# Memory values 2 ahead of the mixer's output projection, memory keys 2 behind it, and an order laid out with the DMA queue as an engine

## The chip, the cores and the metric

One core of one Trainium2 chip runs one program. The time is device microseconds (us) of one execution. Engines: TensorE (PE in the profile, its weight loads PEld), VectorE (DVE), ScalarE (ACT), GpSimd (POOL) and SyncE (SP), which here only issues DMAs.

## The reference, cut to what matters

One layer of a streaming encoder on 512 prompt tokens and 64 sample tokens, 1024 features wide, in float32:

```python
x = x + mixer(rmsnorm(x))                  # gated DeltaNet and GLA branches, merged, then merged @ w_o
k, v = m @ w_k, m @ w_v                    # m = rmsnorm(mem_prompt), 256 memory tokens, 4 heads of 256
x = x + (softmax(q @ k.T / 16) @ v) @ w_mo # q = rmsnorm(x) @ w_mq, head by head
x = x + conv_ffn(rmsnorm(x))               # up, causal convolution, silu gate, down
```

The memory's keys and values (`k`, `v`) depend on `mem_prompt` and the weights alone, not on `x`, so their tiles can stand anywhere ahead of the attention head that reads them. They are outputs too (`o_mk`, `o_mv`).

## The kernel before, in words

Every float32 matrix product is made of three fp32r matmuls: each operand is split into a high part and the rest (`h`, `lo`), and high by high, high by rest and rest by high are summed in one PSUM bank. A 128 x 1024 weight tile comes from DRAM in a raw buffer (`wr`, 512 KB, a DMA issued on SP); ACT casts it to `h`, and `lo` is made in one of two ways. "Summed": ACT writes the negated high part and a DMA issued on POOL adds the weight from DRAM on top (`accumulate`, the rows `w<-wt` on POOL). Otherwise: ACT casts and DVE subtracts (`w<-wr,w`, `w<-ws,w`).

The output projection of the mixer (`wo`), the gates, the attention's output projection and most of the up projection work on pairs of tiles with seven products in place of eight (`products`, L1643): P1, P2, P3, Q4, Q5, Q6, Q7. Each product is 12 matmuls over 288 columns into one of three PSUM banks of the pair (bank a for P1, Q6, Q7 and Q4, b for Q5 and P3, c for P2). When a product is done, `wo_finish` (L1964) has DVE add the bank into the residual tile `x[m]` (`x<-sm,x`), and the next product on the same bank has to wait for that. The weights of P1, P2 and Q4 are quarters of the two raw tiles, made the summed way; those of Q5, Q6, P3 and Q7 are sums and differences of quarters, which DVE forms first (`ws`, from `wr`), then ACT casts and DVE subtracts.

The residual `x` has been overwritten by then, so `x_again` (L1953) loads it afresh, 8 tiles of 288 KB.

The stretch around the change is the list `ATT` (L123): one entry after another on TensorE. `("mk", i)` is one head's keys (two tiles of 24 matmuls, DVE evacuates them to `kraw`, which is stored to `o_mk` and split into `kvh` and `kvl`); `("mv", i)` is one head's values (48 matmuls in one bank, ACT evacuates to `vraw`, stored to `o_mv` and split likewise); `("wo", 0)` is all 28 products of the output projection; `("mq", i)` are queries. In the list, keys 2 stand directly ahead of `wo`, values 2 directly behind it.

The order of every engine's instructions is laid out ahead of time by `Driver` (L250). It runs through the program once, gives each instruction a start from costs per engine (`FIXED`, `PACE`, L255), and emits them in the order of these starts; on the chip each engine then runs its own list in order, and waits by semaphores. DMAs are in the same plan: `load` (L381) and `store` (L387) place a transfer on one resource "D" and put its issue 2.2 us ahead of that; `accumulate` (L393) is the DMA issued on POOL. The time at which the planner thinks that a load has landed decides how early ACT's and DVE's work on it stands in their lists. Issues on SP are in order as well: an issue that waits for its data (a store) or for a free buffer (a load, there are 5 raw buffers) holds up all behind it. `AFTER` (L126) says how many tiles of the down projection follow each pair of the up projection.

All recorded instructions have the line of one helper (L291), so the profile is read by tile names.

Of the kernel before, what the change touches and what calls it, by code (L numbers as in the profile page):

```python
# [14 lines left out]
ALU = mybir.AluOpType  # L15
# [3 lines left out]
D = 1024  # L19
# [18 lines left out]
HOP = 0.2  # L38
BACK = 6.0
MARGIN = 0.3  # L40
NWARM = 11


# [23 lines left out]
def weight_order():  # L67
# [7 lines left out]
    seq += [("out", m) for m in range(max(NB, 4), 8)]  # L75
    for kd, i in ATT:
        if kd == "wo":
# [22 lines left out]
def product_order(pairs, late=False):  # L100

    seq = []
    for i, pair in enumerate(pairs):
        now = [(pair, p) for p in (("P1", "P2", "Q5", "Q6", "P3", "Q7") if late and i == 0 else
                                   ("P1", "Q5", "Q6", "P3", "Q7", "P2", "Q4") if i == len(pairs) - 1 else
                                   ("P1", "Q5", "Q6", "P2", "P3", "Q7"))]
        if i:
            now.insert(2, (pairs[i - 1], "Q4"))  # L110
        seq += now
    return seq
# [7 lines left out]

WPAIRS = [(("wo", m), ("wo", m + 1)) for m in range(0, 8, 2)]

ATT = [("mk", 0), ("mv", 0), ("mv", 1), ("mk", 1), ("mk", 2), ("wo", 0), ("mv", 2), ("mk", 3), ("mq", 0), ("mq", 1), ("mq", 2), ("mq", 3), ("mv", 3)]  # L123
MPAIRS = [(("mo", m), ("mo", m + 1)) for m in range(2, 8, 2)]
JS = 4
AFTER = {7: 2, 8: 2, 9: 2, 10: 2, 13: 2, 14: 2, 15: 2, 16: 2, 20: 2, 21: 2}  # L126


def up_pair(j):
# [3 lines left out]
def ffn_order():  # L133

    seq, old = [("up", j) for j in range(JS)], []
    for j in range(JS, NJ):
# [3 lines left out]
        for i, q in ((j, "P1"), (j - 1, "Q7"), (j, "Q5"), (j, "P2"), (j - 1, "Q4"), (j, "Q6"), (j, "P3")):  # L140
            if i >= JS:
                seq.append(("upx", (i, q)))
        n = AFTER.get(j, 0)
        seq, old = seq + old[:n], old[n:]
# [36 lines left out]
def free(ap):  # L181
    n = 1
    for d in ap.shape[1:]:
        n *= d
    return n


class Engine:


    def __init__(self, drv, key, eng):
        self.drv, self.key, self.eng = drv, key, eng
# [4 lines left out]
    def weigh(self, calls):  # L197
        cost, aps, outs = 0.0, [], []
        for name, args, kw in calls:
# [5 lines left out]
            else:  # L205
                twice = self.key == "V" and len(ins) == 1 and self.port([(name, args, kw)])
                cost += self.drv.FIXED[self.key] + n * self.drv.PACE[self.key] * (0.5 if twice else 1.0)
            cost += 0.06 * (name == "scalar_tensor_tensor" or self.key == "V" and a[0].shape[-1] <= 128 and any(v.space == bass.MemoryType.PSUM for v in a[1:]))
# [41 lines left out]
class Driver:  # L250
# [1 line left out]

    FIXED = dict(V=0.15, A=0.17, G=0.2, D=0.01)  # L255
    PACE = dict(V=1 / 960, A=1 / 1180, G=1 / 465, D=512 / 320e3)

    def __init__(self, pe, sync):
        self.pe, self.sync = pe, sync
        self.chains = []  # L260
        self.done = set()
        self.now = 0.0
        self.half = self.type = None
        self.last = 0.0
        self.swapped = 0.0
        self.wrote = {}
        self.seen = {}
        self.ringed = {}
        self.busy = dict(V=[], A=[], G=[], D=[], port=[])
        self.ring = {}  # L270
        self.pending, self.fresh = set(), set()
        self.heap = []
        self.count = 0
        self.waiting = []
# [98 lines left out]
    def note(self, key, cost, outs, aps, fns, port=False):  # L373
# [4 lines left out]
        self.last = max(self.last, end)  # L378
        self.put(start, fns)

    def load(self, out, in_):  # L381
        cost = self.FIXED["D"] + free(out) * self.PACE["D"]
        start = self.place("D", max(self.ready_at(out), self.latest(self.seen, out)) + 2.2, cost)
        self.mark(self.wrote, start + cost, [out])
        self.put(start - 2.2, [(self.sync.dma_start, (out, in_), {})])

    def store(self, out, in_, issuer=None):  # L387
        cost = self.FIXED["D"] + free(in_) * self.PACE["D"]
        start = self.place("D", self.ready_at(in_) + 2.2, cost)
        self.mark(self.seen, start + cost, [in_])  # L390
        self.put(start - 2.2, [((issuer or self.sync).dma_start, (out, in_), {})])

    def accumulate(self, out, in_, issuer):  # L393

        issue = self.place("G", self.open([out], []), 1.0)
        cost = self.FIXED["D"] + 2 * free(out) * self.PACE["D"]
        end = self.place("D", issue + 2.0, cost) + cost + 1.0
        self.mark(self.wrote, end, [out])
        self.put(issue, [(issuer.dma_start, (out, in_), dict(accum_op=ALU.add))])

    def hold(self, fn, cost, args, kw):
        out, ins = args[0], args[1:]
# [38 lines left out]
    def advance(self, c):  # L441
        self.last = self.now
        r = next(c[1])
        if r is None:
            c[0] = self.last + MARGIN
        elif isinstance(r, list):
            c[0] = self.ready_at(*r) + MARGIN
        elif r != WAIT:
# [53 lines left out]
def tile_trunk(ctx, tc, xT, memT, wt, wd, vec, cst, w0, wgate, st_gdn, st_conv, st_gla, st_ffn, ckT, cv,  # L502
# [3 lines left out]
    V, A, G = Engine(drv, "V", nc.vector), Engine(drv, "A", nc.scalar), Engine(drv, "G", nc.gpsimd)  # L506
# [15 lines left out]
    def nm(s):  # L522
        cnt[0] += 1
        return f"{s}{cnt[0]}"
# [234 lines left out]
    for k in range(KT):  # L759
# [3 lines left out]
        if k in WPART:  # L763
            i, a, b = WPART[k]
# [917 lines left out]
    def xslot(i, s="x"):  # L1682

        return drv.rotate(f"F{i}", 1, fp.tile([P, SLOT], F32R if s != "x" else F32, tag=f"F{i}", name=nm(s), bufs=1))


    def main():
# [52 lines left out]
        for k in range(KT + 1):  # L1740
            for i, ps in enumerate(first2):
                j = k - i
# [210 lines left out]
        def x_again(m):  # L1953

            for i in (m, m + 1):
                x[i] = xslot(i)
                DMA(x[i][:, 0:T], xT[:, i, :])
# [4 lines left out]
        out = []  # L1962

        def wo_finish(pair, prod, a, b, c):  # L1964
            m = pair[0][1]
            xx, scale = (x[m], 0.5) if prod in ("P1", "Q6", "P3", "P2") else (x[m + 1], -0.5)
            half = N1 if prod in ("P1", "P2", "Q4") else N2
            V.scalar_tensor_tensor(xx[:, half], b if prod in ("Q5", "P3") else c if prod == "P2" else a, scale, xx[:, half],
                                   op0=ALU.mult, op1=ALU.add)
            if prod == ("P2" if m == 6 else "P3"):  # L1970
                drv.spawn(c_norm(m, C_GMEM, acc, out))
            elif prod == "Q4":
                drv.spawn(c_norm(m + 1, C_GMEM, acc, out))

        def c_norm(m, gcol, acc_, out_):
            yield [x[m]]
            sq_acc(acc_, x[m], m == 0)
            drv.done.add(("sq", m))
            if drv.ready(*(("sq", i) for i in range(8))):
                drv.spawn(c_rstat("n2", [(acc_, 0)], 4, True, 2.0))  # L1980
            while not drv.ready("wo"):
                yield WAIT
            out_.append((m, norm_prep(x[m], vcol(gcol + m))))
            drv.done.add(("norm", gcol, m))

        for kd, i in ATT:
            if kd == "mk":
                yield from mem_keys(i)
            elif kd == "mv":
                if i == 0:  # L1990
                    for j in range(0, 8, 2):
                        x_again(j)
                yield from mem_values(i)
            elif kd == "wo":
                yield tuple(("wop1", m) for m in range(1, 8, 2))
                yield from products(WPAIRS, [wops[m] for m in range(1, 8, 2)], wo_finish, tuple(("wops", m) for m in range(1, 8, 2)))
                drv.done.add("wo")
            else:
                if i == 0:
                    yield tuple(("norm", C_GMEM, m) for m in range(8))  # L2000
                    xs = xs_of([p for _, p in sorted(out, key=lambda t: t[0])])
                ckr, cvr = slot("ckr"), slot("cvr")
                DMA(r4(ckr[:, 0:512], 256), ckT[:, 2 * i:2 * i + 2, :])
                DMA(r4(cvr[:, 0:512], 256), cv[:, 256 * i:256 * i + 256].rearrange("(a p) d -> p a d", p=P))
                N["ks", i], N["vs", i] = split(ckr), cvr
                for m in (2 * i, 2 * i + 1):
                    b = []
                    yield from tile_proj("mq", m, xs, b)
                    if m == 0:
# [248 lines left out]
        for kd, i in FFN[:-1]:  # L2258
            if kd == "up":
                j = i  # L2260
# [22 lines left out]
            elif kd == "dn1":  # L2283
                m, p = i
# [85 lines left out]
        late, early = [(256, TP, 0), (TP, T, 256)], [(0, 128, 0), (128, 256, 128)]  # L2370
# [213 lines left out]
```

## Time and profile before

| | |
|---|---|
| median of 3 runs | 1089.2 us (1089.12 to 1092.17) |
| the profiled execution | 1091.1 us, its span (first to last instruction) 1089.3 us |
| PE busy | 1077.1 us, 99% of the span, 8278 matmuls |
| PEld busy | 1045.6 us |
| DVE / ACT / POOL busy | 748.4 / 705.9 / 363.1 us |
| DMA | 172.00 MB, mean 158 GB/s; SP's queue 98.26 MB, POOL's 71.84 MB |
| mean granted TensorE clock | 0.997 |

A row of a timeline gives the start, the duration until the last of a merged group ends, the engine, what is written and read, the count, and in brackets how long the engine stood idle before and who released it. The rows are pipelined: a matmul over 288 columns has a duration of 0.30 us, but the next one starts 0.13 us later. A row of windows gives, for a stretch, its length, each engine's busy time with its count, then the granted share of the TensorE clock, the share of the 16 DMA engines and GB/s.

### The profile page before, as it was taken

Reading aid. Unit: us, or ns where it says so; the run is one execution under the profiler, and the core shown is the slowest. Engines: PE = TensorE matmul, PEld = TensorE weight load, DVE = VectorE, ACT = ScalarE, POOL = GpSimd, SP = SyncE. Lnnn points to the kernel's source line nnn. Section 1 sums busy time; section 2 is a strip of 40 time slices with the busy share of each in tenths; the row PEclk is TensorE's granted clock in tenths of the full one; section 3 lists DMA queues with packets and bytes.
Section 4 is the critical chain, followed back from the end, with each engine's and each line's share of the span. In section 5 each row is a group of like instructions: output and inputs, shape, how many; then the busy total and the mean of one; then the engine's idle time right before and its main releaser. Section 6 shows DMA issues by size and latency. Waiting matters only on the chain.

```text
span 1089.3 us, 21589 instructions
## 1 busy us (share of the span) xinstructions
PE 1077.1 (99%) x8278; PEld 1045.6 (96%) x8278; DVE 748.4 (69%) x1460; ACT 705.9 (65%) x1404; POOL 363.1 (33%) x578
## 2 busy tenths in 40 slices
PE   9999999999999999989999999999999999999997
PEld 8999989998988999989999999999999999999997
DVE  6666845776756676886835767767877776778565
ACT  6675546564747577465755668767876776677645
POOL 1243216133624333123410125444343333332224
PEclk9999999999999999999999999999999999999999
DMA  9666345253337889686685258777789688788834
GB/s 302 148 155 149 60 102 138 60 123 83 83 79 150 199 223 194 243 243 163 154 241 148 49 123 194 176 167 150 168 194 196 146 212 186 172 169 183 201 77 112
DMA packets 68040, 172.00 MB, mean 158 GB/s; under 512 B 7905, under 2 KB 14177, under 8 KB 67937
## 3 DMA queue, kind: packets, MB, share of 16 engines
q0 software_dynamic: 30672, 71.84, 38.4%
q1 hardware_dynamic: 36976, 98.26, 27.6%
q8 instruction: 65, 1.06, 0.4%
q10 hardware_dynamic: 288, 0.52, 0.1%
q14 instruction: 39, 0.31, 0.1%
HBM read 158.15 MB, written 5.37 MB: 150 GB/s over the span
## 4 chain that ended last, share of the span: by engine, by line
PE 95%; DVE 1%; DMA 1%; ACT 1%; issue 0%; SPq 0%; ACTq 0%; DVEq 0%
PE sm L291 95%; DMA wr<-wt 1%; DMA x<-xT 0%; DVE w L291 0%; DVE acl L291 0%; ACT w L291 0%; DVE ql L291 0%; DVE ws L291 0%; SPq L291 0%; ACT ach L291 0%; ACT ao L291 0%; ACT vraw L291 0%; DVE q L291 0%; DVE xl L291 0%; ACT xh L291 0%
## 5 line engine op out<-in xcount | busy, mean ns | idle before, releaser
L291 PE MATMUL sm<-xh,w 128*128 128x290 f32 (+3 forms) x2304 | 445.4, 300 | 0.5 <-ACT w L291 0.4
L291 PEld LDWEIGHTS sm<-xh,w 128*128 128x128 f32 x2304 | 356.0, 189 | 5.1 <-issue 1.7
L291 PE MATMUL sm<-xl,w 128*128 128x290 f32 (+3 forms) x1152 | 270.2, 296 | 0.3 <-DVE xl L291 0.2
L291 POOL DMA_DIRECT2D w<-wt x153 | 135.4, 898 | 373.8 <-ACT w L291 284.2
L291 PE MATMUL sm<-ach,w 128*128 128x256 f32 (+1 forms) x1216 | 232.3, 297 | 3.8 <-DVE x L291 3.4
L291 PEld LDWEIGHTS sm<-xl,w 128*128 128x128 f32 x1152 | 200.5, 188 | 0.8 <-DVE xl L291 0.8
L291 PEld LDWEIGHTS sm<-ach,w 128*128 128x128 f32 x1216 | 191.2, 189 | 4.6 <-ACT w L291 3.6
L291 ACT CAST w<-wr 128x512 fp32r<-128x512 f32 (+5 forms) x207 | 158.7, 769 | 19.6 <-PE sm L291 18.1
L291 ACT ACTIVATE w<-wr 128x512 fp32r<-128x512 f32 (+5 forms) x186 | 143.0, 770 | 22.3 <-PE sm L291 19.1
L291 PE MATMUL sm<-acl,w 128*128 128x256 f32 (+1 forms) x608 | 147.1, 296 | 0.3 <-DVE acl L291 0.3
L291 ACT CAST w<-ws 128x512 fp32r<-128x512 f32 (+1 forms) x132 | 78.5, 603 | 47.9 <-DVE ws L291 27.4
L291 PEld LDWEIGHTS sm<-acl,w 128*128 128x128 f32 x608 | 108.1, 189 | 0.5 <-DVE acl L291 0.5
L291 DVE TENSOR_TENSOR w<-ws,w 128x512 fp32r<-128x512 f32 (+1 forms) x104 | 75.2, 731 | 20.5 <-ACT w L291 18.3
L291 DVE SCALAR_TENSOR_TENSOR fc<-fu,vec,fc 128x578 f32<-128x578 f32 x88 | 70.5, 815 | 3.0 <-ACT fc L291 2.9
L291 PE MATMUL sm<-sh,w 128*128 128x290 f32 x288 | 61.2, 297 | 0.0
L291 DVE TENSOR_TENSOR x<-x,sm 128x320 f32<-128x320 f32 (+3 forms) x95 | 38.7, 436 | 30.8 <-PE sm L291 30.5
L291 POOL DMA_DIRECT2D w<-wd x33 | 29.0, 899 | 64.9 <-ACT w L291 58.0
L291 ACT ACTIVATE fc<-fu,vec 128x578 f32<-128x578 f32 x44 | 38.1, 871 | 16.9 <-POOL fu L291 16.4
L291 PEld LDWEIGHTS sm<-sh,w 128*128 128x128 f32 x288 | 47.6, 189 | 0.0
L291 PE MATMUL sm<-oh,w 128*128 128x256 f32 (+1 forms) x256 | 44.7, 295 | 0.0
L291 DVE TENSOR_TENSOR ws<-ws,wr 128x512 f32<-128x512 f32 (+1 forms) x64 | 42.9, 670 | 1.1
L291 POOL DMA_DIRECT2D w<-ws x27 | 23.6, 874 | 50.7 <-ACT w L291 50.2
(388 smaller groups left out, 1958.4 us busy)
## 6 DMA issues: line engine op xcount, KB each, us to landing
wr<-wt SPq DMA_DIRECT2D x130, 512.0 KB, 5.8
w<-wt POOLq DMA_DIRECT2D x52, 512.0 KB, 6.5
w<-wt POOLq DMA_DIRECT2D x101, 256.0 KB, 6.1
w<-ws POOLq DMA_DIRECT2D x27, 256.0 KB, 5.2
x<-xT SPq DMA_DIRECT2D x16, 288.0 KB, 5.9
wr<-wd SPq DMA_DIRECT2D x8, 448.0 KB, 5.3
w<-wd POOLq DMA_DIRECT2D x8, 448.0 KB, 7.1
wr<-wt SPq DMA_DIRECT2D x12, 256.0 KB, 4.7
```

Of the source, the lines that this page charges most:

```text
L291: fn(*args, **kw)
```

## The change

The layout of the work changes in four places, and the planner's account of DMAs in one:

- `ATT`: values 2 change places with keys 2, so `("mv", 2)` stands ahead of `wo` and `("mk", 2)` behind it.
- The first pair of `wo` runs its products as P1, Q5, P2, Q6, P3, Q7 in place of P1, P2, Q5, Q6, P3, Q7.
- `x_again` loads only x[0] to x[3] when values 0 begin; x[4], x[5] are loaded when P1 of the first pair, x[6], x[7] when P1 of the second pair is handed to the planner.
- `AFTER` loses the entry of pair 20: two tiles of the down projection move behind pair 21.
- The planner: SP becomes an engine "S" on which an issue takes 0.55 us; a transfer of a 128 x 1024 tile takes 1.43 us on "D" from 2.0 us after the issue, and lands 1.0 us later; a store is issued 1.0 us after its data are ready (outputs y excepted). Before, a load counted as landed 2.2 us + 1.65 us after its issue, and issues cost nothing. An accumulating DMA is charged 1.2 in place of 2 transfers.

```diff
+STORE = 1.0
+ISSUE, LATENCY, LANDING = 0.55, 2.0, 1.0
...
-        now = [(pair, p) for p in (("P1", "P2", "Q5", "Q6", "P3", "Q7") if late and i == 0 else
+        now = [(pair, p) for p in (("P1", "Q5", "P2", "Q6", "P3", "Q7") if late and i == 0 and pair[0][0] in ('wo',) else
+                                   ("P1", "P2", "Q5", "Q6", "P3", "Q7") if late and i == 0 else
...
-ATT = [("mk", 0), ("mv", 0), ("mv", 1), ("mk", 1), ("mk", 2), ("wo", 0), ("mv", 2), ("mk", 3), ("mq", 0), ("mq", 1), ("mq", 2), ("mq", 3), ("mv", 3)]
+ATT = [("mk", 0), ("mv", 0), ("mv", 1), ("mk", 1), ("mv", 2), ("wo", 0), ("mk", 2), ("mk", 3), ("mq", 0), ("mq", 1), ("mq", 2), ("mq", 3), ("mv", 3)]
...
-AFTER = {7: 2, 8: 2, 9: 2, 10: 2, 13: 2, 14: 2, 15: 2, 16: 2, 20: 2, 21: 2}
+AFTER = {7: 2, 8: 2, 9: 2, 10: 2, 13: 2, 14: 2, 15: 2, 16: 2, 21: 2}
...
-    FIXED = dict(V=0.15, A=0.17, G=0.2, D=0.01)
-    PACE = dict(V=1 / 960, A=1 / 1180, G=1 / 465, D=512 / 320e3)
+    FIXED = dict(V=0.15, A=0.17, G=0.2)
+    PACE = dict(V=1 / 960, A=1 / 1180, G=1 / 465, D=0.0014)
...
+    def moved(self, issued, ap, times=1.0):
+
+        cost = times * free(ap) * self.PACE["D"]
+        return self.place("D", issued + LATENCY, cost) + cost
+
     def load(self, out, in_):
-        cost = self.FIXED["D"] + free(out) * self.PACE["D"]
-        start = self.place("D", max(self.ready_at(out), self.latest(self.seen, out)) + 2.2, cost)
-        self.mark(self.wrote, start + cost, [out])
-        self.put(start - 2.2, [(self.sync.dma_start, (out, in_), {})])
+        at = self.place("S", max(self.ready_at(out), self.latest(self.seen, out)) + HOP, ISSUE)
+        self.mark(self.wrote, self.moved(at + ISSUE, out) + LANDING, [out])
+        self.put(at, [(self.sync.dma_start, (out, in_), {})])
...
+        at = self.place("S" if issuer is None else "A", self.ready_at(in_) + (HOP if in_.tensor.name.startswith("yo") else STORE), ISSUE)
+        self.mark(self.seen, self.moved(at + ISSUE, in_) + LANDING, [in_])
+        self.put(at, [((issuer or self.sync).dma_start, (out, in_), {})])
...
         def wo_finish(pair, prod, a, b, c):
             m = pair[0][1]
+            if prod == "P1" and m < 4:
+                x_again(m + 4)
...
-                    for j in range(0, 8, 2):
+                    for j in range(0, 4, 2):
                         x_again(j)
```

What it does to the engines' lists, at the three places that matter below. SP's list from the load of the first pair's first raw tile on; `wr1149` and `wr1150` are the first pair's raw tiles, `wr1171` and `wr1172` the second pair's. Before:

```order
L291 DMA wr1149_6011<-wt 128x1024
L291 DMA o_mv<-vraw1130_5925 128x2x256
L291 DMA wr1150_6012<-wt 128x1024
L291 DMA o_mk<-kraw1142_6004 128x2x256
L291 DMA wr1171_6128<-wt 128x1024
L291 DMA wr1172_6129<-wt 128x1024
L291 DMA o_mk<-kraw1163_6086 128x2x256
L291 DMA wr1190_6307<-wt 128x1024
L291 DMA wr1191_6308<-wt 128x1024
L291 DMA wr1207_6414<-wt 128x1024
```

SP's list now, from the same tile on; here the second pair's raw tiles are `wr1172` and `wr1173`, and `x1168` to `x1194` are x[4] to x[7]:

```order
L294 DMA wr1149_6008<-wt 128x1024
L294 DMA o_mv<-vraw1119_5849 128x2x256
L294 DMA wr1150_6009<-wt 128x1024
L294 DMA o_mv<-vraw1130_5925 128x2x256
L294 DMA x1168_6173<-xT 128x576
L294 DMA x1169_6174<-xT 128x576
L294 DMA o_mk<-kraw1142_6001 128x2x256
L294 DMA wr1172_6177<-wt 128x1024
L294 DMA wr1173_6178<-wt 128x1024
L294 DMA o_mv<-vraw1159_6083 128x2x256
L294 DMA wr1187_6263<-wt 128x1024
L294 DMA wr1188_6264<-wt 128x1024
```

The first pair's second raw tile moved from behind the second store of values to ahead of it; the second pair's tiles still stand behind the store of keys 1; two loads of `x` came in.

DVE's list in the first pair of `wo`, from the read of P1's bank on. Bank names: `sm1177` is bank a, `sm1185` bank b, `sm1183` bank c. Before:

```order
L291 SCALAR_TENSOR_TENSOR x1113_5839<-sm1177_6165,x1113_5839 128x288
L291 TENSOR_TENSOR w1169_6126<-ws1170_6127,w1169_6126 128x512
L291 TENSOR_TENSOR kvl1176_6164<-kraw1163_6086,kvh1175_6163 128x512
L291 TENSOR_TENSOR ws1179_6187<-wr1172_6129 128x512
L291 TENSOR_TENSOR ws1182_6190<-ws1179_6187,wr1171_6128 128x512
L291 TENSOR_TENSOR w1178_6186<-ws1179_6187,w1178_6186 128x512
L291 TENSOR_TENSOR w1181_6189<-ws1182_6190,w1181_6189 128x512
L291 SCALAR_TENSOR_TENSOR x1113_5839<-sm1183_6191,x1113_5839 128x288
L291 SCALAR_TENSOR_TENSOR x1114_5840<-sm1185_6210,x1114_5840 128x288
L291 SCALAR_TENSOR_TENSOR x1113_5839<-sm1177_6165,x1113_5839 128x288
```

And now; `sm1167` is bank a, `sm1180` bank b, `sm1182` bank c:

```order
L294 SCALAR_TENSOR_TENSOR x1115_5845<-sm1167_6153,x1115_5845 128x288
L294 TENSOR_TENSOR w1170_6175<-ws1171_6176,w1170_6175 128x512
L294 SCALAR_TENSOR_TENSOR x1116_5846<-sm1180_6185,x1116_5846 128x288
L294 TENSOR_TENSOR ws1176_6181<-wr1173_6178 128x512
L294 TENSOR_TENSOR ws1179_6184<-ws1176_6181,wr1172_6177 128x512
L294 TENSOR_TENSOR w1175_6180<-ws1176_6181,w1175_6180 128x512
L294 TENSOR_TENSOR w1178_6183<-ws1179_6184,w1178_6183 128x512
L294 SCALAR_TENSOR_TENSOR x1115_5845<-sm1182_6207,x1115_5845 128x288
L294 TENSOR_TENSOR ws1184_6228<-ws1179_6184,wr1172_6177 128x512
L294 SCALAR_TENSOR_TENSOR x1115_5845<-sm1167_6153,x1115_5845 128x288
```

The read of bank b, on which P3 waits, moved from behind four operations on the second pair's raw tiles to ahead of all of them, and the operation on keys 2 (`kvl1176`) left.

POOL's list of accumulating DMAs: `w1151` is P1 of the first pair; `w1173` before and `w1174` now are P1 of the second pair; `w1180` before and `w1177` now Q4 of the first. Before:

```order
L291 DMA w1151_6013<-wt 128x512
L291 DMA w1157_6048<-wt 128x512
L291 DMA w1173_6130<-wt 128x512
L291 DMA w1180_6188<-wt 128x512
L291 DMA w1184_6209<-wt 128x512
L291 TENSOR_TENSOR ws1187_6230<-ws1182_6190,wr1171_6128 128x512
```

And now:

```order
L294 DMA w1151_6010<-wt 128x512
L294 DMA w1155_6049<-wt 128x512
L294 DMA w1177_6182<-wt 128x512
L294 DMA w1174_6179<-wt 128x512
L294 DMA w1181_6206<-wt 128x512
L294 DMA w1189_6265<-wt 128x512
```

P1 of the second pair moved from the third to the fourth place, behind Q4 of the first pair, and the sum that POOL formed went to DVE.

More of the change, by code (lines that the diff above doesn't have):

```diff
@@ L268, in __init__ @@
         self.ringed = {}
-        self.busy = dict(V=[], A=[], G=[], D=[], port=[])
+        self.busy = dict(V=[], A=[], G=[], D=[], S=[], port=[])
         self.ring = {}
@@ L379, in note @@
         self.put(start, fns)
+    def moved(self, issued, ap, times=1.0):
+        cost = times * free(ap) * self.PACE["D"]
+        return self.place("D", issued + LATENCY, cost) + cost
     def load(self, out, in_):
-        cost = self.FIXED["D"] + free(out) * self.PACE["D"]
-        start = self.place("D", max(self.ready_at(out), self.latest(self.seen, out)) + 2.2, cost)
-        self.mark(self.wrote, start + cost, [out])
-        self.put(start - 2.2, [(self.sync.dma_start, (out, in_), {})])
+        at = self.place("S", max(self.ready_at(out), self.latest(self.seen, out)) + HOP, ISSUE)
+        self.mark(self.wrote, self.moved(at + ISSUE, out) + LANDING, [out])
+        self.put(at, [(self.sync.dma_start, (out, in_), {})])
     def store(self, out, in_, issuer=None):
[L388 to L391, printed above, removed]
+        at = self.place("S" if issuer is None else "A", self.ready_at(in_) + (HOP if in_.tensor.name.startswith("yo") else STORE), ISSUE)
+        self.mark(self.seen, self.moved(at + ISSUE, in_) + LANDING, [in_])
+        self.put(at, [((issuer or self.sync).dma_start, (out, in_), {})])
     def accumulate(self, out, in_, issuer):
[L395 to L399, printed above, removed]
+        at = self.place("G", self.open([out], []), 0.9)
+        self.mark(self.wrote, self.moved(at + 0.9, out, 1.2) + LANDING, [out])
+        self.put(at, [(issuer.dma_start, (out, in_), dict(accum_op=ALU.add))])
     def hold(self, fn, cost, args, kw):
```

## The prediction

> **What bounds the kernel now.** I read the page's busy times first:
>
> ```profile
> span 1089.3 us, 21589 instructions
> PE 1077.1 (99%) x8278; PEld 1045.6 (96%) x8278; DVE 748.4 (69%) x1460; ACT 705.9 (65%) x1404; POOL 363.1 (33%) x578
> ```
>
> PE is busy for 1077.1 of 1089.3 us, and the change takes no matmul away. So it can win only what PE waits for, and lose only by new waits. The waits of PE come next: releaser, total, times, longest.
>
> ```profile
> PE sm L291 <- DVE x L291: 3.4, 1, 3.4
> PE sm L291 <- ACT ach L291: 0.5, 1, 0.5
> PE sm L291 <- ACT w L291: 0.4, 1, 0.4
> PE sm L291 <- DVE ql L291: 0.3, 1, 0.3
> PE sm L291 <- DVE acl L291: 0.3, 1, 0.3
> PE sm L291 <- DVE xl L291: 0.2, 1, 0.2
> ```
>
> One wait, 3.4 us, is twice as long as all others behind the program's start together (1.7). PE's timeline shows its place. Products follow each other by 1.60 us (479.00 to 480.60), so P3, the fifth of the first pair of `wo`, could begin at 479.00 + 4 x 1.60 = 485.40:
>
> ```profile
> 479.00 1.76 PE L291 MATMUL sm<-hl,w 128*128 128x288 f32 x12
> 480.60 0.30 PE L291 MATMUL sm<-ach,w 128*128 128x288 f32 x1
> ...
> 488.89 0.37 PE L291 MATMUL sm<-ach,w 128*128 128x288 f32 x1 [3.36 <-DVE x L291]
> ```
>
> It waits for DVE's read of its bank. The windows behind it (length; PE, PEld, DVE, ACT, POOL; granted clock, DMA share, GB/s) show a second loss:
>
> ```profile
> 488.90:491.50 2.60, 2.60 (x13) 2.60 (x14) 2.10 (x4) 0.62 (x1) 0.00 (x0) 0.60 1.09 282
> 491.50:493.70 2.20, 2.20 (x14) 2.20 (x14) 0.46 (x1) 1.73 (x3) 0.88 (x1) 0.70 0.97 304
> 493.70:495.30 1.60, 1.60 (x15) 1.60 (x14) 1.06 (x2) 0.24 (x1) 0.00 (x0) 1.00 0.59 102
> ```
>
> The clock granted was 0.60 for 2.60 us and 0.70 for 2.20 us: 2.60 x 0.40 + 2.20 x 0.30 = 1.04 + 0.66 = 1.70 us. The stall costs 3.36 + 1.70 = 5.06 us.
>
> Why did DVE read late? I follow four views backwards. SP's timeline:
>
> ```profile
> 474.98 0.39 SPq L291 DMA_DIRECT2D o_mk<-kraw  x1
> 475.42 1.42 SPq L291 DMA_DIRECT2D wr<-wt  x2
> ```
>
> The landing times of these two loads, each from the DMA issues of its own window (the last column is us from issue to landing):
>
> ```profile
> wr<-wt SPq DMA_DIRECT2D x1, 512.0 KB, 5.8
> ...
> wr<-wt SPq DMA_DIRECT2D x1, 512.0 KB, 6.5
> ```
>
> ACT's timeline:
>
> ```profile
> 481.35 0.63 ACT L291 ACTIVATE w<-wr 128x512 fp32r<-128x512 f32 x1 [1.52 <-DMA wr<-wt]
> ...
> 482.40 0.62 ACT L291 CAST w<-ws 128x512 fp32r<-128x512 f32 x1
> ```
>
> And DVE's:
>
> ```profile
> 480.80 0.46 DVE L291 SCALAR_TENSOR_TENSOR x<-sm,x 128x288 f32<-128x288 f32 x1
> 483.05 0.69 DVE L291 TENSOR_TENSOR w<-ws,w 128x512 fp32r<-128x512 f32 x1 [1.79 <-ACT w L291]
> 483.66 0.68 DVE L291 TENSOR_TENSOR kvl<-kraw,kvh 128x512 fp32r<-128x512 f32 x1
> 484.26 0.68 DVE L291 TENSOR_TENSOR ws<-wr 128x512 f32<-128x512 f32 x1
> 484.98 0.69 DVE L291 TENSOR_TENSOR ws<-ws,wr 128x512 f32<-128x512 f32 x1
> 485.65 2.36 DVE L291 TENSOR_TENSOR w<-ws,w 128x512 fp32r<-128x512 f32 x2
> 487.94 1.17 DVE L291 SCALAR_TENSOR_TENSOR x<-sm,x 128x288 f32<-128x288 f32 x3
> ```
>
> The second pair's raw tiles stand on SP behind the store of keys 1 (474.98) and land at about 481.2 (475.42 + 5.8) and 482.6 (the second is issued within the 1.42 of the row; its middle, 476.1, + 6.5). ACT's head of queue waits 1.52 us for the first, so its cast for the first pair's own weight comes at 482.40, and DVE idles 1.79 us. Then DVE's list holds six operations ahead of the reads, which come at 487.94 in place of 483.
>
> **The change part by part.** *The stall.* Of the seven DVE operations between 480.80 and the read of bank b, one is left ahead of it (the changed order, above); the operation on keys 2 is gone. Bank b is now written from 480.60 to 482.20, as Q5 comes second, and P3 still begins at 485.40. The read can start once DVE has the cast's result; even at the old 483.05, with 0.69 and 0.46, it ends at 484.2, 1.2 us early. So -3.36 - 1.70 = -5.06 us.
>
> What is late next? There are two places. First, Q7 (479.00 + 5 x 1.60 = 487.0) needs bank a, which is read behind all of the second pair's preparation. From the landing at 482.6: four operations by 0.6 to 0.7 (rows 483.66 to 485.65) to 485.3, the read of P2 0.46, another sum 0.69, the read of Q6 0.46: 486.9. This is just in time; a landing later by d costs d. I take 0, and as its bound 1.0, a little over the spread of the two landings (6.5 - 5.8 = 0.7).
>
> Second, P1 of the second pair, at 479.00 + 6 x 1.60 = 488.6. Its low part is needed 8 matmuls in, at 488.6 + 8 x 0.13 = 489.6, and comes by an accumulating DMA that now stands behind Q4's on POOL. Issued as now at about 482.3, it lands after 4.1 us (a quiet place) or 7.8 to 9.3 (this place now):
>
> ```profile
> 482.28 1.75 POOL L291 DMA_DIRECT2D w<-wt  x2 [7.75 <-ACT w L291]
> ```
>
> ```profile
> w<-wt POOLq DMA_DIRECT2D x1, 256.0 KB, 4.1
> ```
>
> ```profile
> DMA to landing us min/median/max: 7.8/8.5/9.3
> ```
>
> That is 486.4 to 491.6, so a wait of 0 to 2.0 us. The quiet place waits 0, the middle of the busy rows (8.5, so 490.8) 1.2; I find nothing that says which it is nearer to, and take the mean, 0.6 us.
>
> The Trainium skill, page "TensorE: Matmul & The Clock Gate", section "Part 1: The HAM clock gate", says the clock halves after an idle window of about 3.4 us and returns after as long a busy one. The trace agrees roughly (3.36 us of idling, then 4.8 us at 0.60 and 0.70, not a half); by that rule the short wait left here would cost itself alone.
>
> *Order of matmuls.* PE's list now changes 239 times, in place of 231, between fp32 matmuls of the gated stage and the others: 4 round trips. Such a place reads:
>
> ```profile
> 343.51 0.29 PE L291 MATMUL sm<-xh,w 128*128 128x288 f32 x1
> 343.63 0.29 PE L291 MATMUL sm<-xl,w 128*128 128x288 f32 x1
> 343.95 1.13 PE L291 MATMUL sm<-vg,kt 64*128 64x128 f32 x8
> ```
>
> 343.63 to 343.95 is 0.32 against 0.13 for a usual step: 0.19 us a trip at most, so 0 to 0.76 us; I take 0.4.
>
> *DVE.* Eight sums move from POOL to DVE: 8 x 0.69 = 5.5 us more on an engine busy 748.4 of 1089.3 us. PE hides them unless they stand ahead of a read it waits for; the only such place found is Q7's above. Cost 0; without that cover, 0.69 each.
>
> *x loads.* Four tiles come later, x[4] to x[7]. The store and load order on SP puts two of them ahead of the store of keys 1, so they delay no raw tile of the second pair unless they share its time on the DMA engines (the third rival).
>
> *AFTER, and the planner's numbers elsewhere.* PE has no wait there to win but the small rows (1.7 in all), and each could come back once: 0, bounds -1.1 and +1.1, as not all sit at one end.
>
> **Sum:** -3.36 - 1.70 + 0.6 + 0.4 = -4.06 us. The profiled execution (1091.1, span 1089.3, 1.8 around it) would go to 1087.0; the median of the runs shown is 1089.2, 1.9 below it, with the same order and so the same stall, and I forecast from it: **1085.1 us**. Ends: -5.06 with the small gains is 1083.0; with 1.0 at Q7 or P1, 0.76 of trips and part of the rest, 1087.0.
>
> **Rivals.** *First: the wait comes back at P1 of the second pair.* The accumulate lands as the slowest now, 9.3: wait 2.0, so 1089.2 - 5.06 + 2.0 + 0.4 = 1086.5, and up to 1.7 more if the clock drops, 1088.2. For: 7.8 to 9.3 now. Against: the quiet row, 4.1.
>
> *Second: the change doesn't do what it says.* The raw tiles still stand behind the store of keys 1, as before. If they hold ACT's head of queue as they do now and the wait moves on to Q7, where bank a is read behind their preparation, by as much as it has now (they would have to land 3.3 us later than now, since Q7 is just in time), the 5.06 stays: 1089.2 + 0.4 = 1089.6. For: the store of keys 1 stands ahead of them in both lists. Against: the operations left DVE's list ahead of the read.
>
> *Third, slower: loads of x collide with the accumulates.* Where all eight x loads run now, between 425 and 444, landings read:
>
> ```profile
> wr<-wt SPq DMA_DIRECT2D x6, 512.0 KB, 13.4
> x<-xT SPq DMA_DIRECT2D x8, 288.0 KB, 7.9
> ```
>
> against a usual raw load and accumulate (the page):
>
> ```profile
> w<-wt POOLq DMA_DIRECT2D x101, 256.0 KB, 6.1
> wr<-wt SPq DMA_DIRECT2D x130, 512.0 KB, 5.8
> ```
>
> A raw load there takes 13.4 / 5.8 = 2.3 times as long. If the moved loads do that to the accumulate, it lands 6.1 x 2.3 = 14.0 us after 482.3, at 496.3: wait 6.7, clock 1.7, so 1089.2 - 5.06 + 6.7 + 1.7 + 0.4 = 1092.9. It decides for slower by over 0.3% from a landing of 13.6 us. Against: only two x loads come near, not eight. The Trainium skill, page "DMA: Bandwidth & Descriptors", section "Issuing engines are not separate DMA queues", says transfers of SP and POOL share the 16 engines and interleave; the trace agrees (8.5 against 4.1), and by it this rival costs as worked out.
>
> **How the numbers follow.** A measurement of this kernel tells 0.3% from no change: 3.27 us, so faster is below 1085.9, slower above 1092.5. Forecast 0.62, first rival 0.16, second 0.10, third 0.12. Of the forecast's own range, 1083.0 to 1087.0, about four fifths lie below 1085.9: faster 0.62 x 0.8 = 0.50; same 0.12 + 0.16 + 0.10 = 0.38; slower 0.12. The range runs from 1083.0 over the second rival and a further 1.0 to 1090.6; it leaves out the third rival and little else.
>
> **What would show it.** Right: P3 begins without a wait, the clock reads 1.00 through the first two pairs, and what is left at Q7 or at the second P1 is under 1 us. Wrong: an accumulate that lands over 9.3 us after its issue, a wait of 3 us or more anywhere in `wo`, or new waits in the gated stage, where SP's list moved most and I put 0.

## The result, and the profile after

| | before | after |
|---|---|---|
| median of 6 runs | 1090.0 us (1088.8 to 1092.7) | 1101.1 us (1100.6 to 1102.8) |
| profiled execution, its span | 1091.1, 1089.3 us | 1100.8, 1099.0 us |
| mean granted clock | 0.997 | 0.996 |

The changed kernel is slower: ratio 1.0093, 95% interval 1.0080 to 1.0105. The forecast was 1085.1 us, in a range of 1083.0 to 1090.6. The head of the page after:

```profile
span 1099.0 us, 21611 instructions
PE 1080.6 (98%) x8278; PEld 1047.8 (95%) x8278; DVE 757.2 (69%) x1468; ACT 704.5 (64%) x1404; POOL 357.2 (32%) x570
```

The matmuls are as many as before, so I look for the loss in PE's waits and its clock. The waits of PE after (releaser, total, times, longest), those that are new or have changed:

```profile
PE sm L294 <- DMA w<-wt: 5.9, 2, 4.0
PE sm L294 <- DVE S L294: 1.1, 1, 1.1
PE sm L294 <- ACT gt L294: 1.1, 2, 0.7
...
PE sm L294 <- DVE gt L294: 0.9, 1, 0.9
...
PE sm L294 <- ACT qh L294: 0.4, 1, 0.4
PE sm L294 <- DMA w<-ws: 0.3, 1, 0.3
...
PE sm L294 <- DVE x L294: 0.2, 1, 0.2
```

The 3.4 us for DVE's read of x have become 0.2. In their place stand two waits for an accumulating DMA, 5.9 us, and a few small ones. To see where the time went, I take the first matmul of each stage from PE's timelines: memory keys, the attention's scores, the up projection, the norm's broadcast (`dg`) and the first one that reads `sl`. Before:

```profile
450.63 0.28 PE L291 MATMUL sm<-mh,w 128*128 128x256 f32 x1
558.25 0.28 PE L291 MATMUL sm<-kvh,qh 128*128 128x256 f32 x1
681.15 0.43 PE L291 MATMUL sm<-xh,w 128*128 128x290 f32 x2
700.06 0.97 PE L291 MATMUL sm<-dg,onesr 128*128 128x512 f32 x4
736.72 0.30 PE L291 MATMUL sm<-sl,w 128*128 128x290 f32 x1
```

And after, with the first matmul of `wo` (479.00 before):

```profile
454.66 0.28 PE L294 MATMUL sm<-mh,w 128*128 128x256 f32 x1
483.08 1.74 PE L294 MATMUL sm<-hl,w 128*128 128x288 f32 x12
561.35 0.28 PE L294 MATMUL sm<-kvh,qh 128*128 128x256 f32 x1
684.88 0.43 PE L294 MATMUL sm<-xh,w 128*128 128x290 f32 x2
708.13 1.23 PE L294 MATMUL sm<-dg,onesr 128*128 128x512 f32 x4
746.30 0.29 PE L294 MATMUL sm<-sl,w 128*128 128x290 f32 x1
```

The differences of neighbouring starts give each stage's length:

| stage | before | after | difference |
|---|---|---|---|
| up to the memory's keys (gated stages) | 450.63 | 454.66 | +4.03 |
| keys, values to the start of `wo` | 28.37 | 28.42 | +0.05 |
| `wo` to the scores | 79.25 | 78.27 | -0.98 |
| attention to the up projection | 122.90 | 123.53 | +0.63 |
| up projection to `dg` | 18.91 | 23.25 | +4.34 |
| `dg` to `sl` | 36.66 | 38.17 | +1.51 |
| from there to the span's end | 352.58 | 352.70 | +0.12 |

The sum is +9.7 us, the difference of the spans. Of that, 4.0 us lie ahead of everything that the list `ATT` moves, and 5.9 us lie about 200 us behind the start of `wo`. Of the attention's 0.63, 0.52 are one new wait for ACT (`qh`, at 603.74, from start to start). Stage lengths of the experiments are made in the same way, each from its own timeline.

**In `wo`** the wait moved on. PE's timeline, POOL's and SP's:

```profile
495.90 0.79 PE L294 MATMUL sm<-hl,w 128*128 128x288 f32 x4 [1.89 <-DMA w<-wt]
```

```profile
486.12 1.75 POOL L294 DMA_DIRECT2D w<-wt  x2 [8.08 <-DVE x L294]
```

```profile
485.59 0.90 SPq L294 DMA_DIRECT2D x<-xT  x2
```

The transfer waited for is the second of POOL's two, P1 of the second pair; the first is Q4's of the first pair. Two loads of x, x[6] and x[7], were issued just ahead of them, at 485.6. The landing times of POOL's two after their issue, and the window behind the wait in which the clock dropped:

```profile
DMA to landing us min/median/max: 7.8/8.5/9.2
```

```profile
496.94:500.35 3.41, 3.41 (x17) 3.41 (x16) 1.99 (x4) 0.45 (x1) 0.00 (x0) 0.50 1.07 299
```

A wait of 1.89 us is followed, 1 us later, by 3.41 us at a granted clock of 0.50: 3.41 x 0.50 = 1.71 us. Together that takes back 3.6 of the 5.06 us won.

**In the up projection** PE waits for the other accumulate:

```profile
707.49 0.80 PE L294 MATMUL sm<-xh,w 128*128 128x290 f32 x4 [4.01 <-DMA w<-wt]
```

POOL's timeline before, with the power operation `rt` of the norm, for which POOL waits for DVE:

```profile
687.35 0.88 POOL L291 DMA_DIRECT2D w<-wt  x1 [1.88 <-ACT w L291]
...
689.86 3.37 POOL L291 TENSOR_TENSOR rt<-rin,mhalf 128x5 f32<-128x5 f32 x1 [1.48 <-DVE rin L291]
693.19 1.81 POOL L291 DMA_DIRECT2D w<-wt  x2
```

And after:

```profile
693.59 4.11 POOL L294 TENSOR_TENSOR rt<-rin,mhalf 128x5 f32<-128x5 f32 x1 [4.31 <-DVE rin L294]
697.66 2.70 POOL L294 DMA_DIRECT2D w<-wt  x3
```

One of three accumulates, that of the weight `w1620`, has moved from ahead of `rt` to behind it. Counted from the first matmul of the up projection it is issued at 12.8 us in place of 6.2 (697.66 - 684.88 and 687.35 - 681.15). It then runs beside two others. The DMA issues, before and after (last column: us to landing):

```profile
w<-wt POOLq DMA_DIRECT2D x1, 512.0 KB, 5.2
```

```profile
w<-wt POOLq DMA_DIRECT2D x1, 512.0 KB, 9.8
```

Behind this wait the clock is at 0.50 for 3.41 us again, 1.71 us more:

```profile
708.56:711.97 3.41, 3.41 (x14) 3.18 (x14) 1.44 (x2) 2.47 (x4) 1.43 (x5) 0.50 1.07 238
```

**In the gated stages** PE has four new waits:

```profile
165.27 0.49 PE L294 MATMUL sm<-S,c 128*128 128x128 f32 x2 [1.12 <-DVE S L294]
305.86 0.34 PE L294 MATMUL sm<-keep,on 64*128 64x64 f32 x2 [0.89 <-DVE gt L294]
352.54 0.40 PE L294 MATMUL sm<-ach,w 128*128 128x288 f32 x1 [0.66 <-ACT gt L294]
424.31 0.40 PE L294 MATMUL sm<-ach,w 128*128 128x288 f32 x1 [0.40 <-ACT gt L294]
```

That is 3.07 us of idling. Measured from start to start against the usual step of such matmuls, they are 1.28, 1.05, 0.82 and 0.56 us, with one of 0.27 at 342.7: 3.98 together, of the stage's 4.03. The first has a plain cause. DVE's and POOL's timelines:

```profile
161.30 3.66 DVE L294 SCALAR_TENSOR_TENSOR z<-zt,z 128x576 f32<-128x576 f32 x1
164.88 0.33 DVE L294 SCALAR_TENSOR_TENSOR S<-S,dl,sm 128x128 f32<-128x128 f32 x1
```

```profile
160.86 1.38 POOL L294 TENSOR_TENSOR tg<-cst,ggh 128x512 fp32r<-128x512 f32 x1
161.88 1.36 POOL L294 TENSOR_TENSOR tg<-cst,ggl 128x512 fp32r<-128x512 f32 x1
162.88 1.45 POOL L294 TENSOR_TENSOR e<-gc 128x576 f32<-128x576 f32 x1
```

The gate z takes 3.66 us beside three POOL operations (the median of its kind is 0.76), and the state S, for which PE waits, stands behind it in DVE's list.

### The profile page after: what moved, and what is told of

Read it like the earlier page. It is cut to its first block, busy times and chain, and to the rows that moved or that the text cites. A ratio compares the mean times of both kernels' runs of the same rounds, so it can differ in the third digit from the quotient of the medians.

```text
span 1099.0 us, 21611 instructions
## 1 busy us (share of the span) xinstructions
PE 1080.6 (98%) x8278; PEld 1047.8 (95%) x8278; DVE 757.2 (69%) x1468; ACT 704.5 (64%) x1404; POOL 357.2 (32%) x570
## 4 chain that ended last, share of the span: by engine, by line
PE 91%; DMA 3%; DVE 2%; ACT 2%; issue 1%; POOL 0%; SPq 0%; POOLq 0%; ACTq 0%; DVEq 0%
PE sm L294 91%; DMA w<-wt 2%; DMA w<-ws 1%; ACT w L294 0%; DVE tu L294 0%; DMA x<-xT 0%; DVE z L294 0%; ACT gt L294 0%; ACT xh L294 0%; DVE w L294 0%; DVE ws L294 0%; ACT cx L294 0%; DVE xl L294 0%; DVE acl L294 0%; DVE x L294 0%
## 5 line engine op out<-in xcount | busy, mean ns | idle before, releaser
L294 DVE TENSOR_TENSOR w<-ws,w 128x512 fp32r<-128x512 f32 (+1 forms) x103 | 71.7, 705 | 24.9 <-ACT w L294 22.9
```

Of the source, the lines that this page charges most:

```text
L294: fn(*args, **kw)
```

## The experiments

Two theories were formed from these traces. Theory A: the planner's new figures cost the time, through the lists that they make, and the layout is good. Theory B: the layout (AFTER, the x loads) costs it. Ratios are to the kernel before on the same chip, with a 95% interval; its median there was 1091.5 us in each of the three groups of runs.

**Layout with the old planner.** The changed kernel, with the planner's figures and its load, store and accumulate as before.

```diff
-    PACE = dict(V=1 / 960, A=1 / 1180, G=1 / 465, D=0.0014)
+    PACE = dict(V=1 / 960, A=1 / 1180, G=1 / 465, D=512 / 320e3)
...
```

> The changed list, the new product order, the split x loads and AFTER, with the old planner's numbers. Theory A (the planner's new numbers cost the time, the layout is good): no wait of 4.0 us at the up projection, no new waits in the gated DeltaNet stage, the 3.4 us wait of wo gone: 1089.5 - 5 + 0.5 = about 1085, between 1083 and 1088. Theory B (the layout costs it, by AFTER and the moved loads): 1097 to 1101, with the 4.0 us wait still there.

1091.5 us, ratio 1.0003 (0.9995 to 1.0012). The 4.0 us wait and the gated stage's waits are gone, as theory A says; but the time lies in neither range, since the whole layout is worth nothing. PE still waits in `wo`, and once more in a later pair:

```profile
489.92 0.37 PE L294 MATMUL sm<-ach,w 128*128 128x288 f32 x1 [3.08 <-DVE x L294]
```

SP's timeline shows why:

```profile
475.12 1.54 SPq L294 DMA_DIRECT2D x<-xT  x2
476.71 0.46 SPq L294 DMA_DIRECT2D wr<-wt  x1
479.78 0.40 SPq L294 DMA_DIRECT2D o_mv<-vraw  x1
480.22 2.30 SPq L294 DMA_DIRECT2D wr<-wt  x3
```

The wait is at Q7 (due 8.0 us after the first matmul of `wo`, at 478.71 + 8.0 = 486.7). Two x loads now stand ahead of the second pair's raw tiles. One tile is issued at 476.7, the other at 480.2, behind the store of values 2.

**The planner alone.** The kernel before, with the planner's figures and its load, store and accumulate as after.

```diff
-    PACE = dict(V=1 / 960, A=1 / 1180, G=1 / 465, D=512 / 320e3)
+    PACE = dict(V=1 / 960, A=1 / 1180, G=1 / 465, D=0.0014)
...
```

> The old list, old product order, old x loads and old AFTER, with the new planner's numbers. Theory A: about 3.5 us lost up to 430 us, as in the changed kernel, and 5.7 us at the up projection, with a stall left in wo: 1089.5 + 9.2 = about 1099, or up to 5 us less if the new numbers alone cure the stall in wo. Theory B: 1088 to 1091.

1095.2 us, ratio 1.0038 (1.0024 to 1.0052). The five places of the gated stages and the wait at the up projection (4.1 us) are there, and 1.5 us are left of the stall in `wo`. So the new figures alone make the kernel slower, while they cure part of the stall.

**One accumulate ahead of `rt`.**

```diff
-        at = self.place("G", self.open([out], []), 0.9)
+        at = self.place("G", self.open([out], []), 0.65 if out.tensor.name.startswith("w1620_") else 0.9)
```

> The changed kernel, with one accumulating DMA (of the weight w1620) ahead of the power operation rt on POOL in place of behind it; nothing else is in another order on any engine. Theory A1 (that place in POOL's list makes the 4.0 us wait at 707 us): the wait and the lower clock behind it go, 1101.1 - 4.0 - 1.7 = 1095.4. Rival A2 (the landing is late because three accumulates and raw loads share the DMA engines, wherever it stands): at most 1 us is won, 1100 to 1101.

1096.7 us, ratio 1.0046 (1.0031 to 1.0061), against 1.0093 of the changed kernel: 0.0047 x 1090 = 5.1 us won by one exchange in POOL's list. A few fills of `fu` changed places with it as well (two of them took 0.13 us in the changed kernel); the lists of the other engines are the same. POOL's timeline:

```profile
691.98 0.88 POOL L294 DMA_DIRECT2D w<-wt  x1 [4.35 <-DVE rin L294]
692.59 3.53 POOL L294 TENSOR_TENSOR rt<-rin,mhalf 128x5 f32<-128x5 f32 x1
```

The accumulate now goes out 8.7 us after the first matmul of the up projection and lands after 6.8. Both stretches of the up projection are back at 18.98 and 36.71 us (18.91 and 36.66 before). A1 is shown. In the plan of the changed kernel the accumulate could start at 689.67 and was charged 0.9 us, and `rt` held POOL from 690.37: it missed the room ahead of `rt` by 0.2 us. In the plan before it was ready 3.7 us ahead of `rt`. The planner charged `rt` 1.12 us; on the chip it takes 3.4 to 4.1 and is waited for ahead of that.

**New list and product order, nothing else.**

```diff
-ATT = [("mk", 0), ("mv", 0), ("mv", 1), ("mk", 1), ("mk", 2), ("wo", 0), ("mv", 2), ...
+ATT = [("mk", 0), ("mv", 0), ("mv", 1), ("mk", 1), ("mv", 2), ("wo", 0), ("mk", 2), ...
...
-        now = [(pair, p) for p in (("P1", "P2", "Q5", "Q6", "P3", "Q7") if late and i == 0 else
+        now = [(pair, p) for p in (("P1", "Q5", "P2", "Q6", "P3", "Q7") if late and i == 0 and pair[0][0] in ('wo',) else
```

> The kernel before with two parts alone: values 2 and keys 2 change places, and the first pair's products go P1, Q5, P2. Old planner, all x loads at values 0, old AFTER. If these two are what cures the stall: 1083 to 1086. If the x loads have to be split for it (they fill the DMA engines ahead of wo), a wait of 2 us or more stays in wo: 1087 to 1090.

1088.4 us, ratio 0.9973 (0.9964 to 0.9982): 2.9 us faster than before. The time is in the second range, but both ranges were counted from 1089.5 us, and the kernel before took 1091.5 on this chip; by the ratio the result would be 1086.6, between the two. Without the x loads in front, both raw tiles go out at 475.5 and 476.1, and land 7.1 and 7.8 us later, at 482.6 and 483.9. DVE's timeline and PE's:

```profile
483.89 0.69 DVE L294 TENSOR_TENSOR ws<-wr 128x512 f32<-128x512 f32 x1 [1.57 <-DMA wr<-wt]
```

```profile
487.08 0.37 PE L294 MATMUL sm<-ach,w 128*128 128x288 f32 x1 [1.70 <-DVE x L294]
489.47 0.37 PE L294 MATMUL sm<-ach,w 128*128 128x288 f32 x1 [0.56 <-DVE x L294]
```

The first wait is P3's again, from 478.86 + 6.4 = 485.3 on: in the lists of the old planner DVE's read of bank b still stands behind the second pair's preparation, which waits for the raw tile until 483.89. The second is Q7's. So list and product order don't cure the stall alone. In the changed kernel the read stands further ahead, and the tiles go out 4.6 us ahead of the first matmul of `wo` (478.50) in place of 3.4: that comes with the new planner.

**Old figures up to 430 us of the plan, new ones behind; and the reverse.** Store and accumulate are switched like load; the reverse run has `self.now >= 430`.

```diff
+    def load(self, *a, **kw):
+        (self.load_old if self.now < 430 else self.load_new)(*a, **kw)
```

> The changed kernel, planned with the old numbers for DMAs up to 430 us of its plan and with the new ones from there. In the gated stage every engine's list is then that of the kernel before. Theory A2 (the five waits of PE up to 430 us, 1.28 + 1.05 + 0.82 + 0.56 + 0.27 = 3.98 us, come from the lists that the new numbers make): 4.0 us less than the changed kernel, a ratio to the kernel before of about 1.0056 in place of 1.0093, with the 4.0 us wait at the up projection still there. Rival (those waits are given back later by slack, and the loss is behind 430 us): less than 1 us won, 1.0085 or more.

> The complement: new numbers up to 430 us of the plan, old ones from there, with the whole changed layout. Theory A2: the run with the old planner had a ratio of 1.0003, and the gated stage adds 4.0 us (0.37%): 1.0040, with no 4.0 us wait at the up projection. Rival: 1.0003 to 1.001.

The first: 1097.2 us, ratio 1.0061 (1.0042 to 1.0079); the memory's keys begin at 450.67, as before. The second: 1096.0 us, ratio 1.0046 (1.0033 to 1.0059); they begin at 454.76. So the 4.0 us of the gated stages come from the lists that the new figures make there, and nothing behind gives them back.

**No split of the x loads.** The changed kernel with the accumulate ahead of `rt` and all x loads at values 0, once with the old AFTER and once with the new one.

```diff
-            if prod == "P1" and m < 4:
-                x_again(m + 4)
...
-                    for j in range(0, 4, 2):
+                    for j in range(0, 8, 2):
```

> The new planner with the changed list and product order, the one accumulate ahead of rt, all x loads back at values 0, old AFTER. Theory A3 (the two x loads issued at 485.6 and 486.1, just ahead of the accumulate of the second pair's P1, make it land after 9.15 us): the wait of 1.9 us and the 1.7 us of lower clock in wo go, and only the gated stage's 4.0 us and half a us at the end stand against the 5.1 us won: ratio 0.999 to 1.000. Rival (raw loads and other accumulates crowd it anyway): the wait stays, 1.0025 to 1.0035.

> The changed kernel with the accumulate ahead of rt, and all x loads back at values 0; AFTER as changed. Against the run that had both the x loads and AFTER as before (ratio 1.0014) it tells AFTER apart from the x loads. Theory A3 (it was the x loads): 1.0014 again, no wait at the second pair's P1. Rival (AFTER): 1.0046, as with the x loads split.

With the old AFTER 1092.4 us, ratio 1.0014 (1.0006 to 1.0023): the time lies between the two expectations and fits neither, but the wait went, as theory A3 says. With the new one 1091.9 us, 1.0005 (0.9997 to 1.0014), nearer to theory A3 than to its rival. With the split it was 1.0046 (1.0031 to 1.0061). The wait at the second pair's P1 is gone in both, and `wo` takes 74.4 us to the scores (557.74 - 483.36 and 557.49 - 483.11) against 79.25 before: the stall of 4.9 us is cured. The landing of POOL's pair with the new AFTER:

```profile
DMA to landing us min/median/max: 5.8/6.7/7.5
```

against 7.8/8.5/9.2 with x loads ahead of it. The plan has also put P1's accumulate ahead of Q4's again, and the second pair's raw tiles ahead of the store of keys 1 (the first goes out at 473.9 and 473.6 in place of 478.5). These two runs don't part the three. The changed kernel's rows allow an estimate: its first accumulate, Q4's, went out at 486.12 and landed 7.8 us later, at 493.9, and P1 needed its own at 494.0 (495.90 - 1.89). In the first place it would have been just in time even with the x loads ahead of it. Both runs lose 1.0 to 1.4 us behind the first matmul that reads `sl` (354.02 and 353.58 us to the end, against 352.58), which was not followed up. AFTER's effect is not told from zero: the two intervals overlap.

**Stores on POOL.** List and products as above, old planner, stores of keys and values issued by POOL.

```diff
+        issuer = self.pool if in_.tensor.name.startswith(("kraw", "vraw")) else issuer
```

> The run with the new list and product order alone (old planner), with the stores of memory keys and values issued on POOL in place of SP, so that the second pair's raw tiles do not stand behind them. If the stores hold up the raw tiles (issued at 475.4 behind a store at 475.0): they land 2 us or more earlier and the two waits of 1.86 and 0.72 us left in wo go: ratio about 0.9950. If the tiles wait for free raw buffers instead: they are issued as before, ratio 0.9973.

1088.5 us, ratio 0.9979 (0.9970 to 0.9988). In the profile SP issues the raw tiles at 471.8 and 473.0, over 3 us earlier, and the waits in `wo` shrink from 2.2 to 0.6 us; but the time is not told from that of the run without it (0.9973, overlapping). The tiles did stand behind the stores, as the first expectation says; the gain that it forecast (0.9950) does not show.

**New figures from 430 to 560 us alone.** List and products, old x loads and AFTER.

```diff
+        (self.load_old if not 430 <= self.now < 560 else self.load_new)(*a, **kw)
```

> The changed list and product order, all x loads at values 0, old AFTER, planned with the new numbers from 430 to 560 us of the plan alone and the old ones elsewhere. If the parts add up (the new numbers cure the stall in wo where the x loads are out of the way, 4.87 us less between the first matmul of wo and the attention, and cost 4.0 us up to 430 us and 5.8 us around 700 us): 4.9 us less than the kernel before, ratio 0.9955, and less than the 0.9973 of list and product order with the old planner. Rival (the cure needs the lists of the gated stage, where DVE and POOL stand otherwise): a wait of 2 us stays in wo, ratio 0.9975.

1088.4 us, ratio 0.9975 (0.9965 to 0.9986): as its rival said; PE still waits 1.2 us for DVE's read in `wo`, at Q7. The parts don't simply add up. That `wo`'s lists depend on those ahead fits with this, and was not shown. It is faster than the kernel before, and so is the run with list and products alone; the two are not told apart.

**Earlier landings.** The changed kernel with other figures for the issue, the start and the landing:

```diff
-ISSUE, LATENCY, LANDING = 0.55, 2.0, 1.0
+ISSUE, LATENCY, LANDING = 0.0, 2.2, 0.0
```

> The changed kernel with the planner's three figures near the old ones: an issue takes 0 on SP in its plan, a transfer begins 2.2 us later and counts as landed when it ends. If the late landings and the issue times are what makes the bad lists, the five waits of the gated stage and the 4.0 us wait go: ratio 1.001 to 1.002. If it is the rest of the new account (accumulates at 1.2 transfers, a transfer at 1.43 us, no room for loads that wait for a buffer) or any change at all of the lists: the waits stay or others take their place, 1.006 to 1.010.

1091.0 us, ratio 1.0000 (0.9991 to 1.0008): 10 us better than the changed kernel by three numbers. The wait at the up projection shrinks from 4.0 to 0.9 us, though the accumulate is still behind `rt`; it is issued 10.9 us after the first matmul of the up projection in place of 12.8. In `wo`, P1's accumulate goes out ahead of Q4's again, at 484.69, and lands after 6.4 us; PE doesn't wait for it, though the last two x loads are still split off and follow at 486.04. So the split alone doesn't make that wait. In the gated stages 3.2 us are still lost, mostly in waits at other places than in the changed kernel. So with these three figures near the old ones most of the waits behind 430 us are gone; the loss in the gated stages comes from some other part of the account, or from any new order of lists that had none of these waits. Which figure it is stays open: the old accumulate with the new loads, and the reverse, were not tried.

**The state ahead of the gate.**

```diff
+        late = 1 if key == "V" and fns[0][0].__name__ == "scalar_tensor_tensor" and outs[0].tensor.name.startswith("z") and outs[0].tensor.name.endswith("_1970") else 0.0
-        self.put(start, fns)
+        self.put(start + late, fns)
```

> The changed kernel with two neighbours on DVE swapped: the update of the state S, on which PE waits 1.12 us at 165.3, ahead of the gate z, which takes 3.66 us there beside three POOL operations. Theory A2: that wait goes and the first matmul of the memory's keys comes 1.0 to 1.3 us earlier than in the changed kernel (453.66 us behind the first matmul). Rival (the chain behind waits for z as well): 0.3 us or less.

One execution, 1096.9 us, read by its trace. DVE's timeline:

```profile
161.90 0.35 DVE L294 SCALAR_TENSOR_TENSOR S<-S,dl,sm 128x128 f32<-128x128 f32 x1 [0.43 <-PE sm L294]
162.16 3.10 DVE L294 SCALAR_TENSOR_TENSOR z<-zt,z 128x576 f32<-128x576 f32 x1
```

PE does not wait for S any more, and the memory's keys begin at 453.57, 1.09 us earlier, in the range of theory A2. z still takes 3.10 us beside POOL, but PE does not wait for it. That shows the cause of one of the five; the others were not taken apart.

## Why the prediction was wrong

- **The stall (-5.06).** Right. P3 begins without a wait; DVE reads bank b at 486.4, 3.4 us after the first matmul of `wo`, and P3 needs that 6.4 us after it. The clock loss was read too coarsely: it is not 0.60 and 0.70 for 4.8 us but 0.50 for 3.41 us (the last section has the row), which comes to the same 1.70.
- **Q7 (0, bound 1.0).** Right in the changed kernel, and the right place: there DVE reads bank a from 490.54 to 490.99, 7.9 us after the start, as worked out, and PE needs it 8.0 after. Where tiles land later or stand worse, the same place waits: 3.1 us with the layout and the old planner, 1.2 with the new figures from 430 to 560 us.
- **P1 of the second pair (0.6).** The first rival came true with its price: a wait of 1.89 (2.0 forecast) and 1.71 us of clock (1.7), together 3.6 in place of 0.6. That the clock dropped is luck as far as the forecast goes, since the same wait in another run cost nothing more (last section). Two x loads did stand ahead of it, on which the third rival rested, but they were x[6] and x[7]: SP's list as shown above ends one row ahead of them. The landing took 9.2 us, not the rival's 14.0, and how much of it the x loads made is open.
- **Trips (0.4).** The added changes of type lie in the gated stages, where the five delays make 3.98 of the 4.03 us. So nothing is left that shows a cost of the trips.
- **Sums on DVE, x loads, AFTER (0).** At Q7, the one place named for the sums, DVE was in time, so their 0 holds there. AFTER's 0 is not contradicted. The x loads were put at 0 outside the rival. With the lists that the planner makes of them, their split cost 0.0041 x 1090 = 4.5 us with the new planner (1.0046 against 1.0005); with the old one the split and AFTER cost 0.0030 x 1090 = 3.3 us (1.0003 against 0.9973).
- **The failed step** is "PE has no wait there to win but the small rows (1.7 in all), and each could come back once: 0, bounds -1.1 and +1.1". The trace after showed 4.03 us lost in the gated stages, 5.85 at the up projection and 0.63 in the attention: 10.5 us. The experiments put the first on the lists made with the new figures ahead of 430 us, and 5.1 us of the second on one accumulate behind `rt`. The small waits of before bound what a new order can win. They say nothing of what it can lose, since an engine without waits may have had 0.2 us to spare. The prediction counted 239 changes of type and eight sums, and followed the order of the lists in `wo` alone, though the new figures had moved them everywhere: the accumulate behind `rt` stood in POOL's list to be read. It did name new waits in the gated stage as a sign of being wrong, and this sign came.

The arithmetic by the stage table: -0.98 where -4.46 was forecast for `wo` (-5.06 + 0.6), and +10.5 where 0 was, with 0.4 for the trips.

## What to carry to other kernels

A trace without waits bounds the gain of a new order, not its loss. When a planner's cost figures change, go through all its lists, and look first for a transfer that is issued on an engine behind an operation which waits or is far longer on the chip than in the plan (`rt`: 1.12 planned, 3.4 to 4.1 measured). Change the layout and the planner apart: here two parts of the layout alone, list and product order, won 0.27%; the split x loads with AFTER gave that back (1.0003), and the planner's new figures made of it a loss of 0.93%.

## What the runs showed of the hardware

- A wait can cost its clock, or not, and its length doesn't settle it. Where the clock dropped behind a wait of PE it was at 0.50 for 3.41 us, which is 1.71 us lost, in the kernel before (3.36 us of idling) as behind both long waits of the changed kernel (1.89 and 4.01; rows above). Before:

```profile
489.41:492.82 3.41, 3.41 (x16) 3.41 (x16) 2.05 (x4) 1.66 (x3) 0.12 (x1) 0.50 1.09 285
```

 The run with the accumulate first has the changed kernel's wait at the same place (1.84 us), and the layout with the old planner waits 3.08 us at Q7; behind both the clock stayed at 1.00:

```profile
495.82:499.23 3.41, 3.41 (x25) 3.41 (x26) 2.14 (x4) 0.62 (x1) 0.00 (x0) 1.00 1.07 284
```

```profile
489.92:493.33 3.41, 3.41 (x26) 3.41 (x27) 2.83 (x6) 1.99 (x5) 0.37 (x1) 1.00 1.10 286
```

 That the first of these executions was 1094.0 us where the median of its kernel is 1096.7 fits with a clock that drops in some executions alone, which was not shown. The planner alone waits 4.08 us at the up projection and has two such stretches in a row, 6.83 us at 0.50 from 702.39 on. The Trainium skill, page "TensorE: Matmul & The Clock Gate", section "Part 1: The HAM clock gate", asks for an idle window of about 3.4 us; the 1.89 us here disagree with that.
- A DVE operation of 0.76 us took 3.66 and 3.10 us beside three POOL operations in a row, and ended 0.6 us behind the last of them (161.30 + 3.66 = 164.96, and 162.88 + 1.45 = 164.33). The kernel before has the same at another place: 3.05 us beside two POOL operations, from 225.71 on, and 0.6 us behind the last. So the slow operation is not new; where it stands now, PE waits for the state behind it.
